# Encoder layer: the fourth tile's norm ahead of the first products, a split between the first MLP pair's prompt products, and weight loads in eight pieces beside the dilated heads

## The chip, the cores and the metric

The kernel runs on one core of a Trainium2 chip. The metric is the device time of one execution in microseconds (us). Names of engines: TensorE (PE) does the matrix products and the transposes, ScalarE (ACT) activations and copies out of the product banks, VectorE (DVE) and GpSimd (POOL) the elementwise work, SyncE (SP) issues most of the loads and stores. Each engine runs its own list of instructions in order, and waits where an operand, a buffer or a transfer isn't ready.

## The reference, cut to what matters

One encoder layer on a sequence of 1024 tokens (sample) and one of 256 (prompt), 1024 channels, everything in float32. An input projection gives queries, keys and values of two attention branches and two sets of gates; the branches are merged through the gates, projected, added to the input, and followed by an MLP of width 4096 and a last norm.

```python
def _layer(x, rel_bias, g_mix, w_in, b_gate, ...):
    h = _rmsnorm(x, g_mix)
    z = h @ w_in
    ...
    gates = jax.nn.sigmoid((z[..., o6:] + b_gate).astype(jnp.float32)).astype(x.dtype)
    ...
    o_a, _ = _banded_attention(qa, ka, va, A_WINDOW, 1, rel_bias[:, :A_HEADS], sink)
    o_b = _dilated_mixture(qb, kb, vb, rel_bias[:, A_HEADS:])
    merged = gates[:, :, 0] * (o_a.reshape(b, S, A_Q) @ w_branch_a) + gates[:, :, 1] * (o_b @ w_branch_b)
    x = x + merged @ w_out
    h = _rmsnorm(x, g_mlp)
    return x + jnp.square(jax.nn.relu(h @ w_up)) @ w_down
```

`_dilated_mixture` is attention of 12 heads in three groups with strides of 1, 4 and 16 tokens, each within a window. The outputs are the two sequences after a last `_rmsnorm`.

## The kernel before

**Tiling.** The 1280 tokens are ten tiles of 128 rows: 0 to 7 are the sample, 8 and 9 the prompt. A float32 operand of a product is split in two parts, `hi` (a rounded copy, made by ACT) and `lo` (the rest, `src - hi`, made by DVE), and one product is three matrix products: hi·hi, hi·lo and lo·hi. So a weight goes through a load (`raw`), ACT (`whi`) and DVE (`wlo`) before PE can use it.

**Seven products.** The sample's part of the large projections runs by Strassen's method in Winograd's form: two column blocks of 128 weights make a pair, and the four quarters of the pair are combined to `ta` and `tb` (L389, four subtractions of halves) and multiplied in seven steps (`seven`) with seven combinations of the activations. The order of the steps in a pair is A11, A12, the prompt's product, S2, S3, S1, A22, S4, and the prompt's second product. `right_pair` (L370) is a generator that makes the weights of the next pair: first the loads, then the splits and subtractions, one piece of work for each `next`. The pair before calls it between its own steps.

**Order.** Nearly all parts of the program run in an order written out by hand (`manual_schedule` on all engines): what stands first in the code stands first in each engine's list. The edits change this order or the loads at three places.

*The start* (values stage, L824 to L860). `square(t)` (L732, L734) sums the squares of tile t and takes the root on ACT, `scale(t)` (L738, L739) makes the normed rows `xn` on DVE, and `turn(t)` transposes them on PE and splits the result in `hhi` (ACT, L765) and `hlo` (DVE, L767); for tiles 0 to 3 four plain copies `a` follow on ACT (L778, L779). PE then multiplies tile after tile with the value weights (L794). The tiles `xt` are loaded by SP at the very start.

*The pairs beside the dilated heads* (`pair`, L1016). There are 14 pairs of columns of the input projection. The last five (`MIXED` = 9, `late` true) run beside the dilated attention: after each step of a pair, `beside` gives the attention generator `attention_b` a turn, in which it issues loads of values (`v`, from `scr_v`, L524), computes scores (`sc`, L537) and products (`pv`, L582), and issues loads of queries and keys (`qk`, from `scr_qb` and `scr_kb`, L509 and L512) for a later turn. All these loads and the weight loads (L377) go through SP in one order. Where a load's buffer isn't free yet, or an earlier transfer of the small set of semaphores in rotation hasn't landed, SP waits, and so does everything behind it. Four of these pairs load weights for the next one, two loads of 512 KB each between S2 and S3.

*The first pair of the MLP* (`up`, L1895, with j = 0). It computes its prompt products at the end instead of after A12, so that they come after the first two steps of the next pair (`begin`). `relu2` writes the squared positive part in two ACT operations; for each prompt product that is two blocks of 128 columns and four small operations (`prompt_out`). Then POOL makes four sums (L1946 to L1949) and SP stores the seven results. The weights of pair 1 are made with the subtractions on DVE (`vector` is true for j = 1), and `steps_of(b, 2)` at the head of the next `up` makes the next splits.

Of the kernel before, what the change touches and what calls it, by code (L numbers as in the profile page):

```python
# [15 lines left out]
P = 128  # L16
D = 1024
KC = D // P
# [19 lines left out]
A11, A12, S2, S3, S1, A22, S4 = range(7)  # L38
# [59 lines left out]
def encoder_kernel(  # L98
# [5 lines left out]
    nc = tc.nc  # L104
# [31 lines left out]
    def bank(tag, name=None):  # L136
        return psum.tile([P, 512], F32, name=name or tag, tag=tag, bufs={"mm": 3, "sc": 2, "pt": 2, "pv": 1}[tag])
# [185 lines left out]
    def steps_of(gen, n):  # L323
        for _ in range(n):
            next(gen, None)
# [34 lines left out]
    def seven(ps, which, right, sub, first=True, last=True, mid=None):  # L360
        six(ps, [left(which, k) for k in range(4)], each(right, sub), first, last, mid)
# [5 lines left out]
        six(ps[:, :NP], lefts, each(part, None), True, True, mid)  # L367
        return ps

    def right_pair(cols, out, make=wslot, vector=False):  # L370

        raw = [make("raw", (P, KC, P)) for _ in range(2)]
        for i in range(2):
            nc.sync.dma_start(raw[i], cols[i])  # L377
        yield

        def part(src, shape):  # L380
            out.append((wslot("whi", shape, F32R), wslot("wlo", shape, F32R)))
            yield from split_steps(*out[-1], src)

        b11, b21, b12, b22 = raw[0][:, :4], raw[0][:, 4:], raw[1][:, :4], raw[1][:, 4:]
        if vector:
            yield from part(raw[0], (P, KC, P))
        ta, tb = make("ta", (P, 2, 4, P)), make("tb", (P, 2, 4, P))
        for o, x, y in ((tb[:, 0], b12, b11), (ta[:, 1], b22, b12), (ta[:, 0], b22, tb[:, 0]), (tb[:, 1], b21, ta[:, 0])):
            (nc.vector if vector else nc.gpsimd).tensor_tensor(o, x, y, op=ALU.subtract)  # L389
            if vector:  # L390
                yield
        if not vector:
            yield
            yield from part(raw[0], (P, KC, P))
        for src, shape in ((ta, (P, 2, 4, P)), (tb, (P, 2, 4, P)), (raw[1], (P, KC, P))):
            yield from part(src, shape)
# [272 lines left out]
    with ExitStack() as pre:  # L669
# [59 lines left out]
        def square(t):  # L729
            xn[t] = slot("xn")  # L730
            ss = small.tile([P, 1], F32, name="ss")
            nc.scalar.activation(xn[t], xs[t], AF.Square, accum_out=ss)  # L732
            sds[t] = small.tile([P, 1], F32, name="sd")
            nc.scalar.activation(sds[t], ss, AF.Sqrt, bias=eps, scale=1.0 / D)  # L734

        def scale(t):
            rs = small.tile([P, 1], F32, name="rs")
            nc.vector.reciprocal(rs, sds.pop(t))  # L738
            nc.vector.scalar_tensor_tensor(xn[t], xs.pop(t), rs, gm, op0=ALU.mult, op1=ALU.mult)  # L739
# [102 lines left out]
        square(2)  # L842
        scale(2)
        next(turns[0], None)
        pss = [bank("mm", "v") for _ in range(2)]
        for t, i in ((0, 0), (0, 1), (1, 0), (1, 1), (0, 2), (1, 2), (0, 3), (1, 3)):
            if (t, i) == (0, 3):
                next(turns[2])
            values(t, 0, pss[t], range(2 * i, 2 * i + 2))
        next(turns[2])  # L850
        square(3)
        next(turns[1], None)
        scale(3)
        square(4)
        next(turns[2], None)
        nc.vector.memset(tab[BUCKETS:, :], NEG)
# [51 lines left out]
    if True:  # L908
# [104 lines left out]
        def pair(b, parts, cols, nxt, hooks, beside, late):  # L1013

            one, two = (out_of(c) for c in cols)
            x, y = bank("mm", "x"), bank("mm", "y")
            np_ = []
            nb = right_pair([w_in3[:, :, c : c + P] for c in nxt], np_, wslot, late) if nxt else iter(())  # L1020

            def halfway(gen=None):
                beside()
                if late:
                    steps_of(gen or nb, 2)

            def behind():
                beside()
                if not late:
                    steps_of(b, 2)  # L1030

            one.begin()
            seven(x, A11, parts[0], 0, last=False, mid=lambda: halfway(b))
            c1 = stage("c", n=2)
            nc.scalar.activation(c1, x, AF.Copy, scale=one.scale)
            behind()
            seven(y, A12, parts[0], 1, mid=lambda: halfway(b))
            one.sum(0, 512, y, c1)
            behind()
            pa = prompt(parts[0], "mm", lambda: halfway(b))  # L1040
            if not late:
                next(nb, None)
            next(hooks, None)
            one.direct(NS, NP, pa)
            beside()
            seven(x, S2, parts[1], 0, False, False, beside)
            c2 = stage("c", n=2)
            nc.scalar.activation(c2, x, AF.Copy, scale=one.scale)
            behind()
            if late:  # L1050
                next(nb, None)
            z = bank("mm", "z")
            seven(z, S3, parts[1], 1, last=False, mid=beside)
            c7 = stage("c", n=2)
            nc.scalar.activation(c7, z, AF.Copy, scale=two.scale)
            two.begin()
            beside()
            next(hooks, None)
            seven(x, S1, parts[2], 0, False, False, beside)
            two.sum(512, 512, x, c7)  # L1060
            beside()
            if not late:
                steps_of(nb, 3)
            next(hooks, None)
            seven(z, A22, parts[2], 1, False, mid=halfway)
            one.sum(512, 512, z, c2)
            one.store()
            beside()
            next(hooks, None)
            seven(x, S4, parts[3], 1, False, mid=halfway)  # L1070
            two.direct(0, 512, x)
            beside()
            two.direct(NS, NP, prompt(parts[3], "mm", halfway))
            two.store()
            beside()
            return nb, np_
# [786 lines left out]
    with ExitStack() as pre:  # L1863
# [25 lines left out]
        def up(j, b, parts, hooks):  # L1889

            def prompt_out(ps, dst):
                for i, d in enumerate(dst):
                    relu2(d[:, 512:], ps[:, P * i : P * i + P])  # L1895

            u = [stage(f"u{i}", TH) for i in range(7)]
            u11, u12, u22, u21 = u[A11], u[A12], u[A22], u[S3]
            start = begin(parts)
            if j not in begun:  # L1900
                next(start)
            z = bank("sc", "z")
            nb = np_ = None
            steps_of(b, 2)
            next(hooks, None)
            x, y, c1 = begun[j] if j in begun else next(start)
            relu2_sum(u11[:, :512], y, c1)
            steps_of(b, 2)
            if j:
                pa = prompt(parts[0])  # L1910
            if j + 1 < FF // P // 2:
                np_ = []
                nb = right_up(j + 1, np_)
                next(nb)
            next(hooks, None)
            seven(x, S2, parts[1], 0, False, False)
            c2 = stage("c2", 512)
            nc.scalar.activation(c2, x, AF.Copy)
            if j:
                prompt_out(pa, (u11, u21))  # L1920
            steps_of(b, 2)
            next(hooks, None)
            seven(z, S3, parts[1], 1, last=False)
            c7 = stage("c7", 512)
            nc.scalar.activation(c7, z, AF.Copy)
            if not j:
                steps_of(nb, 2)
            next(hooks, None)
            seven(x, S1, parts[2], 0, False, False)
            relu2_sum(u22[:, :512], x, c7)  # L1930
            next(hooks, None)
            if nb and j:
                steps_of(nb, 3)
            seven(z, A22, parts[2], 1, False)
            relu2_sum(u21[:, :512], z, c2)
            next(hooks, None)
            if not j:
                *_, begun[1] = begin(np_)
            seven(x, S4, parts[3], 1, False)
            relu2(u12[:, :512], x)  # L1940
            next(hooks, None)
            if not j:
                steps_of(nb, 4)
                prompt_out(prompt(parts[0]), (u11, u21))
            prompt_out(prompt(parts[3], "sc"), (u12, u22))
            nc.gpsimd.tensor_tensor(u[S1], u21, u22, op=ALU.add)  # L1946
            nc.gpsimd.tensor_tensor(u[S2], u[S1], u11, op=ALU.subtract)
            nc.gpsimd.tensor_tensor(u[S3], u11, u21, op=ALU.subtract)
            nc.gpsimd.tensor_tensor(u[S4], u12, u[S2], op=ALU.subtract)  # L1949
            for i in (A11, S1, A22, S2, S3, A12, S4):  # L1950
                nc.sync.dma_start(scr_u[j // 4][:, i, j % 4, :], u[i])
            next(hooks, None)
            return nb, np_
# [47 lines left out]
```

## Time and profile before

| | us |
|---|---|
| timed runs | 1692.21, 1692.16, 1690.64 |
| median | 1692.16 |
| the profiled execution's own time | 1693.05 |
| its span, from the first to the last instruction | 1691.3 |

A row of a timeline gives the start in us, the length in us, the engine, the line, the operation and its operands (out<-in), and how often it stands there in a row; in brackets the idle time of the engine just before it and what ended that. Rows of SP show issues, not transfers. Rows such as "raw<-in_w_in_dram SPq DMA_DIRECT2D x2, 512.0 KB, 8.3" give the number of loads issued in a stretch, the size of one and the median us from issue to landing. Matrix products are pipelined, so that starts can lie closer together than a product is long.

### The profile page before, as it was taken

The numbers are of one execution on the slowest core, as the hardware profiler recorded it, in microseconds if no ns is written. First come the engines' busy times: TensorE is split into PE (matmuls) and PEld (weight loads), VectorE is DVE, ScalarE is ACT, GpSimd is POOL, SyncE is SP. The second block draws the span as 40 slices with busy tenths as digits, with TensorE's granted clock in tenths as the row PEclk, the third lists the DMA queues.
The fourth block names the chain that finished last, engine by engine and source line by source line (L and its number), as shares of the span: only waits on it lengthen the run. The fifth ranks groups of instructions, "written<-read, shape, count | busy, mean of one in ns | idle before, by whom it ended". The sixth has DMA issues, their size and how long they took to land.

```text
span 1691.3 us, 24932 instructions
## 1 busy us (share of the span) xinstructions
PE 1670.7 (99%) x9268; PEld 1414.9 (84%) x9268; DVE 950.1 (56%) x1548; ACT 721.3 (43%) x1489; POOL 514.9 (30%) x404
## 2 busy tenths in 40 slices
PE   8999999999999999999999999999999999999998
PEld 7898888887788888888888888888887888888886
DVE  6733233455563565667378445455457767667575
ACT  6332323356562656654176333333334333333345
POOL 1312212212112472200100556455556322314150
PEclk9999999999999999999999999999999999999999
DMA  7416562567666893845121443343346744633333
GB/s 246 151 57 125 134 136 75 162 192 200 182 196 193 219 245 100 289 136 189 41 85 58 159 159 118 121 159 130 116 152 250 280 152 157 209 106 116 119 119 124
DMA packets 224408, 260.35 MB, mean 154 GB/s; under 512 B 29568, under 2 KB 154288, under 8 KB 224288
## 3 DMA queue, kind: packets, MB, share of 16 engines
q1 hardware_dynamic: 214976, 235.60, 43.9%
q0 software_dynamic: 7936, 20.54, 5.6%
q10 hardware_dynamic: 1376, 2.62, 0.4%
q8 instruction: 73, 1.20, 0.3%
q14 instruction: 47, 0.39, 0.1%
HBM read 173.03 MB, written 90.92 MB: 156 GB/s over the span
## 4 chain that ended last, share of the span: by engine, by line
PE 90%; DVE 4%; ACT 2%; DMA 2%; issue 1%; POOL 1%; SPq 0%; DVEq 0%; ACTq 0%; POOLq 0%
PE dn L347 20%; PE x L347 18%; PE mm L192 14%; PE z L347 9%; PE v L794 6%; PE mm L347 5%; PE y L347 5%; PE sc L347 2%; PE pv L347 2%; PE sc L537 1%; PE pv L1170 1%; PE pv L582 1%; PE pt L569 1%; PE pt L1155 1%; PE sc L1131 1%
## 5 line engine op out<-in xcount | busy, mean ns | idle before, releaser
L347 PE MATMUL dn<-dhi,ulo 128*128 128x512 f32 x448 | 175.7, 392 | 4.3 <-DVE ulo L186 4.3
L347 PE MATMUL dn<-dlo,uhi 128*128 128x512 f32 x448 | 175.2, 391 | 0.0
L347 PE MATMUL dn<-dhi,uhi 128*128 128x512 f32 x448 | 175.1, 391 | 0.0
L347 PE MATMUL x<-chi,wlo 128*128 128x512 f32 x424 | 167.3, 395 | 1.7 <-DVE wlo L314 1.6
L347 PE MATMUL x<-clo,whi 128*128 128x512 f32 x424 | 165.7, 391 | 0.1
L347 PE MATMUL x<-chi,whi 128*128 128x512 f32 x424 | 165.1, 389 | 0.0
L314 DVE TENSOR_TENSOR wlo<-ta,whi 128x1024 fp32r<-128x1024 f32 x30 | 55.7, 1857 | 179.1 <-ACT whi L312 179.1
L314 DVE TENSOR_TENSOR wlo<-raw,whi 128x1024 fp32r<-128x1024 f32 x60 | 92.5, 1541 | 96.7 <-ACT whi L312 96.7
L389 POOL TENSOR_TENSOR tb<-raw 128x512 f32<-128x512 f32 x25 | 32.7, 1308 | 364.4 <-DMA raw<-in_w_in_dram 147.8
L347 PEld LDWEIGHTS dn<-dhi,ulo 128*128 128x128 f32 x448 | 84.6, 189 | 23.2 <-DVE ulo L186 5.7
L186 DVE TENSOR_TENSOR ulo<-uraw,uhi 128x1024 fp32r<-128x1024 f32 x56 | 94.3, 1702 | 12.4 <-ACT uhi L185 12.4
L347 PEld LDWEIGHTS dn<-dhi,uhi 128*128 128x128 f32 x448 | 84.7, 189 | 17.8
L347 PEld LDWEIGHTS dn<-dlo,uhi 128*128 128x128 f32 x448 | 84.7, 189 | 17.4
L347 PEld LDWEIGHTS x<-chi,wlo 128*128 128x128 f32 x424 | 79.8, 188 | 18.1 <-DVE wlo L314 1.3
L347 PEld LDWEIGHTS x<-chi,whi 128*128 128x128 f32 x424 | 79.6, 188 | 17.0
L1699 POOL TENSOR_TENSOR t<-raw,t 128x1024 f32<-128x1024 f32 x16 | 47.7, 3001 | 147.0 <-DMA raw<-in_w_down_dram 147.0
L347 PEld LDWEIGHTS x<-clo,whi 128*128 128x128 f32 x424 | 79.8, 188 | 14.8 <-DVE clo L314 0.4
L1853 DVE TENSOR_TENSOR v<-v,dn 128x512 f32<-128x512 f32 x90 | 59.6, 681 | 40.4 <-PE dn L347 37.9
L1946 POOL TENSOR_TENSOR u<-u,u 128x640 f32<-128x640 f32 x16 | 26.1, 1630 | 160.0 <-ACT u L1871 160.0
L347 PE MATMUL dn<-dhi,up 128*128 128x512 f32 x224 | 73.5, 389 | 0.0
L347 PE MATMUL z<-chi,wlo 128*128 128x512 f32 x184 | 72.0, 391 | 0.0
L272 ACT ACTIVATE pt<-pt 128x512 f32<-128x512 f32 (+1 forms) x70 | 37.9, 543 | 79.5 <-PE pt L1155 45.0
(325 smaller groups left out, 4660.9 us busy)
## 6 DMA issues: line engine op xcount, KB each, us to landing
scr_u<-u SPq DMA_DIRECT2D x112, 320.0 KB, 2.6
uraw<-scr_u SPq DMA_DIRECT2D x56, 512.0 KB, 4.5
raw<-in_w_in_dram SPq DMA_DIRECT2D x33, 512.0 KB, 5.4
raw<-in_w_up_dram SPq DMA_DIRECT2D x32, 512.0 KB, 5.2
raw<-in_w_down_dram SPq DMA_DIRECT2D x28, 512.0 KB, 6.6
sg<-scr_g SPq DMA_DIRECT2D x32, 256.0 KB, 6.4
uraw<-scr_u SPq DMA_DIRECT2D x28, 256.0 KB, 4.7
v<-scr_v SPq DMA_DIRECT2D x96, 64.0 KB, 2.7
```

Of the source, the lines that this page charges most:

```text
L186: nc.vector.tensor_tensor(lo, src, hi.bitcast(F32), op=ALU.subtract)
L192: nc.tensor.matmul(ps, a, b, start=i == 0, stop=i == len(seq) - 1)
L272: nc.scalar.activation(out, in_, AF.Copy)
L314: nc.vector.tensor_tensor(lo, src, hi.bitcast(F32), op=ALU.subtract)
L347: nc.tensor.matmul(ps, a, b, start=first and i == 0, stop=last and i == len(seq) - 1, skip_group_check=True)
L389: (nc.vector if vector else nc.gpsimd).tensor_tensor(o, x, y, op=ALU.subtract)
L537: nc.tensor.matmul(at(k, h)[p0 : p0 + nq, :], qk[rows, p0 : p0 + nq], qk[rows, P + P * a : P + P * a + W], start=True, stop=True, skip_gro ...
L569: nc.tensor.transpose(ps[:, P * a : P * a + P], s[:, h, P * k : P * k + P], ident)
L794: nc.tensor.matmul(ps[:, :n], a, b, start=k == 0 and j == 0, stop=k == KC - 1 and j == 2)
L1699: nc.gpsimd.tensor_tensor(o, a, b, op=ALU.subtract)
L1853: nc.vector.tensor_tensor(v, v, ps, op=ALU.add)
L1946: nc.gpsimd.tensor_tensor(u[S1], u21, u22, op=ALU.add)
```

## The change

Three edits, each at one of the places above.

1. In the start, `square(3)` and `scale(3)` stand ahead of the loop over the first products instead of behind it.
2. In `pair`, the weights of the next pair come in eight loads of 128 KB (two of the eight blocks of rows each) instead of two of 512 KB. They are issued one by one: one after the prompt's product, two around S2's second half, two around S3, three around S1. The subtractions and splits behind them keep their places.
3. In `up` with j = 0, two steps of the next pair's weights are made between the two prompt products, instead of later.

```diff
--- before.py
+++ after.py
@@ -367,15 +367,19 @@
         six(ps[:, :NP], lefts, each(part, None), True, True, mid)
         return ps

-    def right_pair(cols, out, make=wslot, vector=False):
+    def right_pair(cols, out, make=wslot, vector=False, step=KC):

         raw = [make("raw", (P, KC, P)) for _ in range(2)]
         for i in range(2):
-            nc.sync.dma_start(raw[i], cols[i])
-        yield
+            for c in range(0, KC, step):
+                nc.sync.dma_start(raw[i][:, c : c + step, :], cols[i][:, c : c + step, :])
+                if step < KC:
+                    yield
+        if step == KC:
+            yield

         def part(src, shape):
             out.append((wslot("whi", shape, F32R), wslot("wlo", shape, F32R)))
@@ -842,15 +846,15 @@
         square(2)
         scale(2)
         next(turns[0], None)
+        square(3)
+        scale(3)
         pss = [bank("mm", "v") for _ in range(2)]
         for t, i in ((0, 0), (0, 1), (1, 0), (1, 1), (0, 2), (1, 2), (0, 3), (1, 3)):
             if (t, i) == (0, 3):
                 next(turns[2])
             values(t, 0, pss[t], range(2 * i, 2 * i + 2))
         next(turns[2])
-        square(3)
         next(turns[1], None)
-        scale(3)
         square(4)
         next(turns[2], None)
         nc.vector.memset(tab[BUCKETS:, :], NEG)
@@ -1017,7 +1021,7 @@
             one, two = (out_of(c) for c in cols)
             x, y = bank("mm", "x"), bank("mm", "y")
             np_ = []
-            nb = right_pair([w_in3[:, :, c : c + P] for c in nxt], np_, wslot, late) if nxt else iter(())
+            nb = right_pair([w_in3[:, :, c : c + P] for c in nxt], np_, wslot, late, 2 if late else KC) if nxt else iter(())

             def halfway(gen=None):
                 beside()
@@ -1028,6 +1032,14 @@
                 beside()
                 if not late:
                     steps_of(b, 2)
+
+            def piece():
+                if late:
+                    next(nb, None)
+
+            def piece_beside():
+                beside()
+                piece()

             one.begin()
             seven(x, A11, parts[0], 0, last=False, mid=lambda: halfway(b))
@@ -1042,24 +1054,27 @@
                 next(nb, None)
             next(hooks, None)
             one.direct(NS, NP, pa)
+            piece()
             beside()
-            seven(x, S2, parts[1], 0, False, False, beside)
+            seven(x, S2, parts[1], 0, False, False, piece_beside)
             c2 = stage("c", n=2)
             nc.scalar.activation(c2, x, AF.Copy, scale=one.scale)
             behind()
-            if late:
-                next(nb, None)
+            piece()
             z = bank("mm", "z")
-            seven(z, S3, parts[1], 1, last=False, mid=beside)
+            seven(z, S3, parts[1], 1, last=False, mid=piece_beside)
             c7 = stage("c", n=2)
             nc.scalar.activation(c7, z, AF.Copy, scale=two.scale)
             two.begin()
             beside()
+            piece()
             next(hooks, None)
-            seven(x, S1, parts[2], 0, False, False, beside)
+            seven(x, S1, parts[2], 0, False, False, piece_beside)
             two.sum(512, 512, x, c7)
             beside()
-            if not late:
+            if late:
+                steps_of(nb, 2)
+            else:
                 steps_of(nb, 3)
             next(hooks, None)
             seven(z, A22, parts[2], 1, False, mid=halfway)
@@ -1942,6 +1957,7 @@
             if not j:
                 steps_of(nb, 4)
                 prompt_out(prompt(parts[0]), (u11, u21))
+                steps_of(nb, 2)
             prompt_out(prompt(parts[3], "sc"), (u12, u22))
             nc.gpsimd.tensor_tensor(u[S1], u21, u22, op=ALU.add)
             nc.gpsimd.tensor_tensor(u[S2], u[S1], u11, op=ALU.subtract)
```

The first place is ACT in the start. Names: `xn,ss<-xt` is the sum of squares, `sd<-ss,eps` the root, `a_...<-tr` the plain copies of a turned tile. Before:

```order
L778 ACTIVATE a_307<-tr 128x2x128
L779 ACTIVATE a_309<-tr 128x2x128
L778 ACTIVATE a_308<-tr 128x2x128
L779 ACTIVATE a_310<-tr 128x2x128
L765 ACTIVATE hhi<-tr 128x2x128 x4
L732 ACTIVATE xn,ss<-xt 128x1024
L734 ACTIVATE sd<-ss,eps 128x1
L778 ACTIVATE a_307<-tr 128x2x128
L779 ACTIVATE a_309<-tr 128x2x128
```

and now:

```order
L782 ACTIVATE a_307<-tr 128x2x128
L783 ACTIVATE a_309<-tr 128x2x128
L782 ACTIVATE a_308<-tr 128x2x128
L783 ACTIVATE a_310<-tr 128x2x128
L736 ACTIVATE xn,ss<-xt 128x1024
L738 ACTIVATE sd<-ss,eps 128x1
L769 ACTIVATE hhi<-tr 128x2x128 x4
L782 ACTIVATE a_307<-tr 128x2x128
L783 ACTIVATE a_309<-tr 128x2x128
```

The sum of squares and the root of the fourth tile, which stood behind the four `hhi` copies of the third, stand ahead of them. On DVE `rs<-sd` and `xn` move ahead of the third tile's `hlo` in the same way.

The second place is SP in the third of the four pairs that load weights (names with numbers are arrays in memory: `scr_qb_120` and `scr_kb_126` the queries and keys of the group without stride, `scr_g` columns of a gate). Before, from the load of queries and keys ahead of the weights:

```order
L923 DMA scr_g_134<-z 128x256
L524 DMA v<-scr_v 128x128 x2
L509 DMA qk<-scr_qb_120 128x128
L509 DMA qk<-scr_kb_126 128x256
L509 DMA qk<-scr_qb_120 128x128
L509 DMA qk<-scr_kb_126 128x256
L377 DMA raw<-in_w_in_dram 128x8x128 x2
L524 DMA v<-scr_v 128x128 x2
L509 DMA qk<-scr_qb_120 128x128
L509 DMA qk<-scr_kb_126 128x256
L509 DMA qk<-scr_qb_120 128x128
L509 DMA qk<-scr_kb_126 128x256
```

and now:

```order
L378 DMA raw<-in_w_in_dram 128x2x128
L927 DMA scr_g_134<-z 128x256
L528 DMA v<-scr_v 128x128 x2
L513 DMA qk<-scr_qb_120 128x128
L513 DMA qk<-scr_kb_126 128x256
L513 DMA qk<-scr_qb_120 128x128
L513 DMA qk<-scr_kb_126 128x256
L378 DMA raw<-in_w_in_dram 128x2x128 x2
L528 DMA v<-scr_v 128x128 x2
L513 DMA qk<-scr_qb_120 128x128
L513 DMA qk<-scr_kb_126 128x256
L513 DMA qk<-scr_qb_120 128x128
```

Where 1 MB was issued ahead of the two loads of `v`, two pieces of 128 KB stand there now, one stands ahead of the store and the group before, and two, then three more, follow behind the next two groups of queries and keys (not shown).

The third place is ACT in the first pair of the MLP, from its prompt products to the next pair's (`pv` and `sc` are the banks of the two prompt products, `c` a copy of a product, kept for a later sum). Before:

```order
L1870 ACTIVATE u_9308<-pv 128x128
L1871 ACTIVATE u_9308<-u_9308 128x128
L1870 ACTIVATE u_9306<-sc 128x128
L1871 ACTIVATE u_9306<-u_9306 128x128
L1870 ACTIVATE u_9310<-sc 128x128
L1871 ACTIVATE u_9310<-u_9310 128x128
L312 ACTIVATE whi<-ta 128x1024
L312 ACTIVATE whi<-tb 128x1024
L1918 ACTIVATE c_9637<-x 128x512
L1870 ACTIVATE u_9578<-pv 128x128
```

and now:

```order
L1885 ACTIVATE u_9332<-pv 128x128
L1886 ACTIVATE u_9332<-u_9332 128x128
L312 ACTIVATE whi<-ta 128x1024
L1885 ACTIVATE u_9330<-sc 128x128
L1886 ACTIVATE u_9330<-u_9330 128x128
L1885 ACTIVATE u_9334<-sc 128x128
L1886 ACTIVATE u_9334<-u_9334 128x128
L312 ACTIVATE whi<-tb 128x1024
L312 ACTIVATE whi<-raw 128x1024
L1933 ACTIVATE c_9665<-x 128x512
```

`whi<-ta` now stands ahead of the four operations on `sc`, and `whi<-raw`, which stood four operations later, follows `whi<-tb`. On DVE the same pair's rows were:

```order
L389 TENSOR_TENSOR tb<-raw,ta 128x512
L314 TENSOR_TENSOR wlo<-ta,whi 128x1024
L1874 TENSOR_TENSOR u_9578<-y,c_9475 128x512
L1875 SCALAR_TENSOR_TENSOR u_9578<-u_9578 128x512
L314 TENSOR_TENSOR wlo<-tb,whi 128x1024
L314 TENSOR_TENSOR wlo<-raw,whi 128x1024
```

and are now:

```order
L393 TENSOR_TENSOR tb<-raw,ta 128x512
L314 TENSOR_TENSOR wlo<-ta,whi 128x1024
L314 TENSOR_TENSOR wlo<-tb,whi 128x1024
L1889 TENSOR_TENSOR u_9606<-y,c_9499 128x512
L1890 SCALAR_TENSOR_TENSOR u_9606<-u_9606 128x512
L314 TENSOR_TENSOR wlo<-raw,whi 128x1024
```

The `wlo` of `tb` stands ahead of the two operations on `u`, the first of which adds `y` and `c`.

## The prediction

> **What bounds the kernel now.** I read the page first, then the list of what TensorE (PE) waits for, then the timelines around those waits.
>
> ```profile
> span 1691.3 us, 24932 instructions
> PE 1670.7 (99%) x9268; PEld 1414.9 (84%) x9268; DVE 950.1 (56%) x1548; ACT 721.3 (43%) x1489; POOL 514.9 (30%) x404
> ```
>
> PE is busy 1670.7 us of a span of 1691.3 us. The diff leaves PE's list of instructions alone, in number and order, so all that it can take away is time in which PE waits: 20.6 us in the whole program, and a large gain is excluded. The other engines are far from full, so work that moves on them costs nothing unless PE waits for it. The list of waits has four on which an edit of the diff bears, and I take them site by site. Each term is the idle time of PE ahead of one row; the row's bracket gives it and what ended it. A stop costs a little more than its idle time: in PE's rows of site 2 below, products that start 0.22 us apart (456.50, 456.72) are followed by a start at 458.96, so 2.24 − 0.22 = 2.02 us are lost for 1.85 us of idle. I add 0.15 us for each stop that goes away whole.
>
> **Site 1, the start: the fourth tile's norm.** Rows of PE:
>
> ```profile
> 26.23 1.06 PE L338 MATMUL tr<-ident,xn 128*128 128x128 f32 x8 [1.10 <-DVE tab L856]
> ```
>
> of ScalarE (ACT):
>
> ```profile
> 21.99 1.21 ACT L765 ACTIVATE hhi<-tr 128x256 fp32r<-128x256 f32 x4 [4.30 <-PE tr L338]
> 23.06 1.08 ACT L732 ACTIVATE xn<-xt 128x1024 f32<-128x1024 f32 x1
> 24.27 0.29 ACT L734 ACTIVATE sd<-ss,eps 128x1 f32<-128x1 f32 x1
> ```
>
> of VectorE (DVE):
>
> ```profile
> 22.68 1.42 DVE L767 TENSOR_TENSOR hlo<-tr,hhi 128x256 fp32r<-128x256 f32 x4 [3.43 <-ACT hhi L765]
> 24.79 1.28 DVE L739 SCALAR_TENSOR_TENSOR xn<-xt,rs,gm 128x1024 f32<-128x1024 f32 x1
> ```
>
> and of the loads of x, issued by SyncE (SP), with their median time from issue to landing:
>
> ```profile
> 4.41 3.68 SPq L682 DMA_DIRECT2D xt<-in_x_sample_dram  x4
> xt<-in_x_sample_dram SPq DMA_DIRECT2D x4, 512.0 KB, 10.9
> ```
>
> The transposes at 26.23 need the fourth tile's `xn`, finished at 24.79 + 1.28 = 26.07 (the label `tab` names a tiny operation that ended next to it). Before that, ACT squares (1.08) and takes the root (0.29), both behind four `hhi` copies that wait for the third tile's transposes. After the change these stand ahead of the `hhi` copies. ACT sat idle 4.30 us there, DVE 3.43 us, so 1.08 + 0.29 = 1.4 us on ACT and then 1.28 us on DVE are covered, if the tile has landed: it is the second of four loads issued over 3.68 us, so about 4.41 + 0.92 + 10.9 = 16.2 us, ahead of ACT's idle time, which runs from 17.7 to 21.99. DVE then ends `xn` near 19.25 + 1.3 to 20.7, six microseconds early, and `hlo` at 22.68 isn't delayed. The whole wait goes: **1.10 + 0.15 = 1.25 us**. If the tile came as late as the copies, the moved work would stand in front of `hhi`, which the third tile's products need, and would cost up to 1.4 us instead; 16.2 against 21.99 rules that out. What is late next is the fifth tile's `xn`, and its `square` moves up with the rest.
>
> **Site 2, the dilated heads: weights in pieces.** SP issues the loads in order, and an issue that waits holds up those behind it. Its rows:
>
> ```profile
> 448.23 1.05 SPq L377 DMA_DIRECT2D raw<-in_w_in_dram  x2
> 449.38 5.00 SPq L524 DMA_DIRECT2D v<-scr_v  x2
> ...
> 454.90 0.42 SPq L509 DMA_DIRECT2D qk<-scr_kb  x1
> 455.85 0.42 SPq L509 DMA_DIRECT2D qk<-scr_kb  x1
> ```
>
> PE's rows there:
>
> ```profile
> 453.11 0.66 PE L582 MATMUL pv<-pt,v 128*64 128x128 f32 x8
> ...
> 456.50 0.39 PE L347 MATMUL z<-hlo,whi 128*128 128x512 f32 x1
> 456.72 0.39 PE L347 MATMUL z<-hhi,whi 128*128 128x512 f32 x1
> 458.96 1.28 PE L537 MATMUL sc<-qk 64*128 64x256 f32 x8 [1.85 <-DMA qk<-scr_kb]
> ```
>
> And the median times from issue to landing, of what was issued in 446 to 449, in 454 to 456, and in 340 to 505:
>
> ```profile
> raw<-in_w_in_dram SPq DMA_DIRECT2D x2, 512.0 KB, 8.3
> qk<-scr_kb SPq DMA_DIRECT2D x2, 128.0 KB, 3.8
> qk<-scr_kb SPq DMA_DIRECT2D x36, 128.0 KB, 3.0
> ```
>
> Two things make this `qk` late. The `v` load ahead of it holds SP for 5.00 us until the products at 453.11 have released its buffer; that stays. And the two weight loads issued at 448.23, 1 MB together, take 8.3 us and are still draining when `qk` goes out, so that it lands after 3.8 us instead of 3.0. After the change only two 128 KB pieces stand there, a quarter of the bytes, and at a quarter of the 8.3 us they are gone before 453. The issues stay at 454.90 and 455.85. The first half of the scores needs the first of these tiles, the second half, 0.64 us on (half of 1.28), the other. Landing in 3.0 us, they are there at 457.9 and 458.85, which lets the scores start between 457.9 and 458.2: 0.75 to 1.06 us saved. Landing in 2.5 us, it is 1.25 to 1.56. If 3.8 is what such a load takes there anyway, nothing is saved. I take **1.0 us**, by the median of all 36 loads of this kind, and leave 0 to 1.9 for the range.
>
> This happens in one of four pairs; in the others the weights cost PE nothing. All four pay for the pieces: 8 issues in place of 2, 24 more in all, at about 0.45 us each on SP (the x2 and x1 rows above: 0.42 to 0.53), or 24 × 0.45 = 11 us of SP, never of PE, unless a `qk` behind them is late. The tightest places, by rows of SP, the landing of what was issued in 400.8 to 401.9, and rows of PE:
>
> ```profile
> 401.30 0.58 SPq L509 DMA_DIRECT2D qk<-scr_kb  x1
> ...
> 417.55 1.95 SPq L512 DMA_DIRECT2D qk<-scr_kb  x1
> ```
>
> ```profile
> qk<-scr_kb SPq DMA_DIRECT2D x1, 128.0 KB, 4.2
> ```
>
> ```profile
> 405.89 1.13 PE L537 MATMUL sc<-qk 64*128 64x256 f32 x8
> ...
> 423.14 0.67 PE L537 MATMUL sc<-qk 64*64 64x128 f32 x16
> ```
>
> At 405.89 the last `qk` left at 401.30 and landed 4.2 us on, at 405.5; the second half of the scores needs it at 406.45, a margin of 0.95. One piece now stands ahead: 0.45 us of SP, and 128 KB more to drain, about 0.5 us at the eighth of 8.3 / 2. That uses the margin up and no more. At 423.14 three pieces stand ahead: 1.35 us of SP, against 417.55 + 1.95 + 2.5 = 422.0 (its issue waited, so I count from its end) and a margin of 1.1 to the start. The wait inside those 1.95 us shrinks when the issue comes later, which gives some of it back. I allow **+0.3 us** for all four pairs; bounds 0 and the sum in the third rival.
>
> [...]
>
> **Site 3, first pair of the MLP: a split between two prompt products.** Rows of ACT, of DVE and of PE:
>
> ```profile
> 926.94 0.28 ACT L1870 ACTIVATE u<-sc 128x128 f32<-128x128 f32 x1 [1.75 <-PE sc L347]
> 927.98 1.04 ACT L312 ACTIVATE whi<-ta 128x1024 fp32r<-128x1024 f32 x1
> ```
>
> ```profile
> 929.05 1.75 DVE L314 TENSOR_TENSOR wlo<-ta,whi 128x1024 fp32r<-128x1024 f32 x1 [4.74 <-ACT whi L312]
> 933.79 0.69 DVE L1874 TENSOR_TENSOR u<-y,c 128x512 f32<-128x512 f32 x1 [2.98 <-POOL u L1948]
> ...
> 935.76 1.21 DVE L314 TENSOR_TENSOR wlo<-tb,whi 128x1024 fp32r<-128x1024 f32 x1
> ```
>
> ```profile
> 930.86 0.50 PE L347 MATMUL x<-chi,wlo 128*128 128x512 f32 x1 [1.08 <-DVE wlo L314]
> ...
> 937.12 0.47 PE L347 MATMUL x<-chi,wlo 128*128 128x512 f32 x1 [0.48 <-DVE wlo L314]
> ```
>
> PE waits twice here for a `wlo`. The first, of `ta`, ends at 929.05 + 1.75 = 930.8, because its `whi` stands on ACT behind four small operations that wait for PE. After the change `whi<-ta` runs in ACT's idle 1.75 us ahead of 926.94 (it needs 1.04) and DVE, idle 4.74 us, follows at once: `wlo` by about 926.3 + 1.2 = 927.5, two microseconds before PE needs it at 930.86 − 1.08 = 929.8. The small operations aren't delayed, since 925.2 + 1.04 is still ahead of 926.94, and POOL starts on time. The second `wlo`, of `tb`, stood on DVE behind `u<-y,c`, which waits 2.98 us for POOL. It now stands in front: `whi` is done by 927.98 + 1.04 = 929.0, `wlo` by 930.3 (1.2 alone) or 932.5 (3.5, twice the slower 1.75, beside POOL); it is needed at 936.6. `u<-y,c` and its partner then go at 933.79 as before, and nothing of PE waits on them there. Both waits go whole: **1.08 + 0.48 + 2 × 0.15 = 1.9 us**.
>
> **The sum.** −1.25 − 1.0 + 0.3 − 1.9 = −3.85 us. The profiled execution took 1693.05 us, so 1689.2 against it; it is the slowest of those shown, 0.9 above the median of 1692.16 of the timed runs, and against that median it is **1688.3 us**, 0.23% faster. About 0.2% (3.4 us) is what a measurement of this kernel can tell from no change, so the forecast lies close above that line.
>
> **The rivals.**
>
> *First: site 2 keeps its wait.* For it: the issue is held by PE's own products at 453.11, which the pieces don't touch, and pieces are in flight there as well. Against: 3.8 us beside a median of 3.0. Then −1.25 − 1.9 + 0.3 = −2.85: 1689.3 us, within 0.2%.
>
> *Second: all four waits go.* If `qk` lands within 2.2 us of its issue and the tight places hold: −1.25 − 2.0 − 1.9 = −5.15: 1687.0 us.
>
> *Third, the other side: pieces make `qk` late.* One mechanism: each piece pushes the `qk` issues behind it by 0.45 us and their data by about 0.5 us, and a `qk` that is later than its margin stops PE. With 0.95 us per piece, three pieces cost 2.85 against the 1.1 us of margin at 423.14, so 1.75 us; one costs 0.95 against the 0.95 at 405.89. At 1.5 us for each pair, a little under that worst place, four pairs make 6 us, and the net is 6 − 1.25 − 1.9 = +2.85: 1695.0 us, slower. It decides from the point where the added delay beats the margin in most pairs. Against: the two 512 KB loads it replaces put the same bytes into the same stretch, and PE doesn't stop in three of four pairs.
>
> **How the numbers follow.** Forecast 0.48 (1688.3), first rival 0.25 (1689.3), second 0.14 (1687.0), third 0.13 (1695.0, with lesser forms from 1691 up). The runs of before differ by 1692.21 − 1690.64 = 1.6 us, so I count ±0.8 about each. Faster by over 0.2% means below 1688.8: 0.34 of the forecast's 0.48, 0.13 of the second, a quarter of the first (0.07): 0.54. Slower by over 0.2%, above 1695.5, is the worse half of the third: 0.07. The rest, 0.39, is within 0.2%. The range goes from 1686.5, half a microsecond below the second rival, to 1691.3, two above the first: it leaves out the third and little else.
>
> **What would show it.** Site 1: no idle time ahead of the transposes after the third pair of products, and `square` in ACT's idle time. Site 3: both `x<-chi,wlo` starts without a bracket, `wlo<-ta` near 1.2 us. Site 2: the wait at 458.96 cut to about 1 us, and no new PE wait on `qk` or on `wlo` between 340 and 505; the landing of `qk` there near 3.0. The prediction is wrong if new waits for `qk` of over 1 us in sum appear, if the raw pieces come too late for their subtractions, or if any of the first and third sites' waits stays.

## The result, and the profile after

The changed kernel took 1688.56 us (median of 15 runs, 1685.87 to 1691.12), the kernel before, run beside it, 1692.45 us (15 runs, 1690.56 to 1695.35). The ratio is 0.9975, with a 95% interval from 0.9968 to 0.9983: by it 4.2 us faster, between 2.9 and 5.4; the medians differ by 3.9. The forecast was 1688.3. The profiled execution took 1688.49 us. From its page:

```profile
span 1686.7 us, 24976 instructions
PE 1669.5 (99%) x9268; PEld 1414.7 (84%) x9268; DVE 952.5 (56%) x1548; ACT 721.6 (43%) x1489; POOL 511.7 (30%) x404
```

The list of what TensorE waits for (us in all, times, longest) is now:

```profile
PE dn L347 <- DVE ulo L186: 4.3, 3, 3.2
PE tr L338 <- DVE xn L743: 1.8, 2, 0.9
PE warm L711 <- POOL ident masks.py:199: 1.4, 1, 1.4
PE mm L192 <- DVE wlo L235: 1.0, 1, 1.0
PE v L798 <- DVE vlo L705: 0.7, 1, 0.7
PE mm L192 <- ACT z L999: 0.5, 1, 0.5
```

The four waits that the edits aim at (`tab`, `qk` and twice `wlo` of L314) are gone. Two new ones stand there, `wlo` of L235 (1.0) and `z` (0.5), both at places that no edit touches, at 702 and 539 us. To see what is chance in this, the time between the starts of the same two TensorE instructions is taken in every profile; a stretch is named by the times at which these stand in the first profile of the kernel before. From that profile to this one the stretch 14–30 us (site 1) lost 16.02 − 14.72 = 1.30 us, 345–510 (site 2) 1.74, and 925–945 (site 3) 2.15; 510–710 grew by 1.80, and 1290–1310, which no edit touches, lost 1.19. Together 4.58 of the 4.6 us between the spans.

**Site 1.** Rows of ACT and of DVE in the changed kernel, and TensorE's transposes:

```profile
17.53 1.08 ACT L736 ACTIVATE xn<-xt 128x1024 f32<-128x1024 f32 x1
...
18.73 0.29 ACT L738 ACTIVATE sd<-ss,eps 128x1 f32<-128x1 f32 x1
21.96 1.21 ACT L769 ACTIVATE hhi<-tr 128x256 fp32r<-128x256 f32 x4 [2.94 <-PE tr L338]
```

```profile
19.34 1.29 DVE L743 SCALAR_TENSOR_TENSOR xn<-xt,rs,gm 128x1024 f32<-128x1024 f32 x1
22.65 1.42 DVE L771 TENSOR_TENSOR hlo<-tr,hhi 128x256 fp32r<-128x256 f32 x4 [2.02 <-ACT hhi L769]
```

```profile
24.95 1.03 PE L338 MATMUL tr<-ident,xn 128*128 128x128 f32 x8
```

The square has no wait of its own, so the tile had landed; `xn` ends at 20.63 (forecast: up to 20.7), ACT's idle time ahead of `hhi` shrinks from 4.30 to 2.94, and `hhi` itself isn't later. The transposes carry no bracket.

**Site 3.** ACT, DVE and PE:

```profile
923.85 1.04 ACT L312 ACTIVATE whi<-ta 128x1024 fp32r<-128x1024 f32 x1
925.70 0.28 ACT L1885 ACTIVATE u<-sc 128x128 f32<-128x128 f32 x1 [0.80 <-PE sc L347]
```

```profile
924.93 1.23 DVE L314 TENSOR_TENSOR wlo<-ta,whi 128x1024 fp32r<-128x1024 f32 x1 [1.87 <-ACT whi L312]
927.81 1.76 DVE L314 TENSOR_TENSOR wlo<-tb,whi 128x1024 fp32r<-128x1024 f32 x1 [1.66 <-ACT whi L312]
932.55 0.69 DVE L1889 TENSOR_TENSOR u<-y,c 128x512 f32<-128x512 f32 x1 [2.98 <-POOL u L1964]
```

```profile
928.38 0.40 PE L347 MATMUL x<-chi,wlo 128*128 128x512 f32 x1
```

`whi<-ta` fills ACT's idle time, both `wlo` are there 2.2 us and more before TensorE asks for them, and the long wait of DVE for POOL (2.98) still stands, with nothing of TensorE behind it. The second `wlo`, which runs while POOL makes its sums, takes 1.76 us, the first, without POOL, 1.23.

**Site 2.** SP in the changed kernel, at the place of the wait:

```profile
447.59 1.57 SPq L378 DMA_DIRECT2D raw<-in_w_in_dram  x2
449.26 0.94 SPq L528 DMA_DIRECT2D v<-scr_v  x2
450.29 0.41 SPq L513 DMA_DIRECT2D qk<-scr_qb  x1
450.80 0.38 SPq L513 DMA_DIRECT2D qk<-scr_kb  x1
```

```profile
456.05 1.13 PE L541 MATMUL sc<-qk 64*128 64x256 f32 x8
```

The wait is gone whole, and not for the reason that the prediction gave: the `v` loads, which held SP for 5.00 us before, now take 0.94, so `qk` (`scr_kb`) leaves at 450.80 instead of 454.90. Of these 4.1 us, 1.3 are the lead that TensorE has from site 1; by the other 2.8 us `qk` is earlier than the products that need it. What of this the pieces did, the experiments tell.

### The profile page after: what moved, and what is told of

Its sections match the earlier page's. It is cut to its first block, busy times and chain, and to the rows that moved or that the text cites. A ratio compares the mean times of both kernels' runs of the same rounds, so it can differ in the third digit from the quotient of the medians.

```text
span 1686.7 us, 24976 instructions
## 1 busy us (share of the span) xinstructions
PE 1669.5 (99%) x9268; PEld 1414.7 (84%) x9268; DVE 952.5 (56%) x1548; ACT 721.6 (43%) x1489; POOL 511.7 (30%) x404
## 4 chain that ended last, share of the span: by engine, by line
PE 91%; DVE 4%; ACT 2%; DMA 1%; issue 1%; POOL 0%; SPq 0%; DVEq 0%; ACTq 0%; POOLq 0%
PE dn L347 20%; PE x L347 18%; PE mm L192 14%; PE z L347 9%; PE v L798 6%; PE mm L347 5%; PE y L347 5%; PE pv L347 3%; PE sc L347 2%; PE pv L1185 2%; PE sc L541 1%; PE pv L586 1%; PE pt L573 1%; PE pt L1170 1%; PE sc L1146 1%
## 5 line engine op out<-in xcount | busy, mean ns | idle before, releaser
L314 DVE TENSOR_TENSOR wlo<-ta,whi 128x1024 fp32r<-128x1024 f32 x30 | 55.2, 1840 | 173.0 <-ACT whi L312 173.0
L314 DVE TENSOR_TENSOR wlo<-raw,whi 128x1024 fp32r<-128x1024 f32 x60 | 90.9, 1516 | 96.3 <-ACT whi L312 96.3
L393 POOL TENSOR_TENSOR tb<-raw 128x512 f32<-128x512 f32 x25 | 32.3, 1290 | 368.4 <-DMA raw<-in_w_in_dram 127.6
L347 PE MATMUL z<-chi,whi 128*128 128x512 f32 x184 | 71.6, 389 | 0.0
```

Of the source, the lines that this page charges most:

```text
L314: nc.vector.tensor_tensor(lo, src, hi.bitcast(F32), op=ALU.subtract)
L347: nc.tensor.matmul(ps, a, b, start=first and i == 0, stop=last and i == len(seq) - 1, skip_group_check=True)
```

## The experiments

Three questions: what each edit is worth alone, whether what stood at site 2 and behind it belongs to the kernels or to one execution, and by what the weight loads reach TensorE.

**Each edit alone, and the whole again.** The first adds the two `square(3)`/`scale(3)` lines of the diff alone, the second the pieces alone, the third `steps_of(nb, 2)` alone; the fourth is the changed kernel unaltered.

> The fourth tile's norm alone. Theory: the wait of 1.10 us ahead of the transposes goes, TensorE is 1.26 us ahead from there on, the other three waits stay: 1.3 us less, ratio 0.9992. By theory A on the later waits (transfers that keep their own time) a part of it is lost again at 702, where the kernel before had about 0.1 us of slack: then 0.1 to 0.5 us in the end. Rival: another wait near the start grows by as much, ratio 1.000.

> The eight pieces alone. Theory from the profile after: the wait of 1.85 us goes whole (2.06 us with its slower restart) and 0.3 us come back at the scores before it: 1.8 us less by 460, ratio 0.9990 if it reaches the end, 0.9996 if the stretch at 702 takes 1.1 us of it. Prediction on record: 0.7 us less. Rival: pieces alone, without the earlier TensorE of the first part, meet a different state of the transfers and a part of the wait stays (0.8 us or more at that place).

> The split between the first MLP pair's prompt products alone. Theory: both waits on wlo (1.08 and 0.48 us) go, 2.1 us with the slower restarts, and nothing behind it is bound by transfers: 2.1 us less at the end, ratio 0.9988, no change at all ahead of 925 us. Rival: the long wait on ulo (3.2 us) takes a part of it: then that wait is 4 us or more and the end only 1 us earlier, ratio 0.9994.

> The changed kernel once more, for a second profile. In the first one TensorE had two waits that the kernel before hasn't: 0.52 us on ScalarE's z<-x at 539.4 and 0.97 us on wlo at 702.3, together 1.5 us given back of what the three sites had won by then. Theory A: they belong to the change (TensorE comes 2.4 to 3 us earlier to stretches whose transfers keep their own time); then both are there again, 0.5 and 1.0 us. Theory B: they are chance in the transfers of one execution; then at least one is gone or of another size. In both the four waits of before (1.10, 1.85, 1.08, 0.48 us) stay away, and the time is 0.9975 of before, within 0.0008.

Measured, against 1692.33 us of the kernel before: norm alone 1690.58, ratio 0.9988 (0.9979 to 0.9997); split alone 1690.54, 0.9986 (0.9977 to 0.9995); pieces alone 1692.21, 0.9997 (0.9988 to 1.0005); the whole again 1687.24, 0.9968 (0.9956 to 0.9981). The profiles are sharper than the times:

```
us between the same TensorE instructions
                      14-30   345-510   510-710   925-945   1290-1310
before                16.02   164.94    200.02    20.11     20.01
norm alone            14.73   163.45    199.14    20.11     18.22
split alone           16.01   163.35    200.61    17.96     18.79
pieces alone          16.02   163.27    201.48    20.09     18.87
changed               14.72   163.20    201.82    17.96     18.82
changed, again        14.72   162.87    200.28    17.96     18.85
```

Sites 1 and 3 are exact: 1.3 and 2.15 us whenever the edit is in, nothing when it isn't. Site 2 isn't. Norm alone and split alone load the weights as before, and the long wait on `qk` isn't there: 0 and 0.29 us at that place instead of 1.85. The two later waits of the changed kernel (0.52 and 0.97) were 0.17 and 0 in its second profile, and 0.51 and 0.47 with the pieces alone: theory B.

**The kernel before once more, and the two other edits without the pieces.**

> The kernel before once more, for a second profile. The stretch from 447 to 465 us (by the first profile's times, at the same instruction of TensorE) took 18.02 us there, with the 1.85 us wait; in the two kernels without pieces (norm alone, split alone) it took 16.24 and 16.44, in the three with pieces 15.96 to 16.36. Theory C: the long wait was chance in the transfers of one execution; then 16.2 to 16.6 us now. Theory D: it belongs to the exact times of this kernel and an earlier or later TensorE avoids it; then about 18.0 us again. The waits at the start (1.10) and of wlo (1.08, 0.48) are there in both.

> The first and third edit without the pieces. Theory C (pieces worth nothing that shows): stretches 385 to 505 as in the changed kernel within 0.4 us, ratio 0.9975 as the whole change. Theory by the prediction's terms: pieces worth 0.7 us, ratio 0.9979; by the first profile's 1.8 us, ratio 0.9986. In all of them 3.4 us less at the two sites.

The kernel before took 1692.0 us, ratio 1.000 (0.999 to 1.001). From 447 to 465 it needed 16.68 us instead of 18.02, with a wait of 0.51 us where 1.85 had been (and one of 0.28 at 412, so that 345–510 took 164.16); TensorE's waits for `wlo` (1.09, 0.51) and ahead of the transposes (1.09) were all there. So most of the 1.85 us was chance in the transfers: theory C. The two edits without the pieces took 1688.3 us, ratio 0.9975 (0.9964 to 0.9986), the same as with them, and 163.41 in the stretch.

**What the loads do to SP.** Two kernels without pieces otherwise (first and third edit are in):

```diff
 (whole loads at the first piece's place)
             one.direct(NS, NP, pa)
+            if late:
+                next(nb, None)
             beside()
...
             behind()
-            if late:
-                next(nb, None)
 (eight pieces in a row at the old place)
-            nc.sync.dma_start(raw[i], cols[i])
+            for c in range(0, KC, step):
+                nc.sync.dma_start(raw[i][:, c : c + step, :], cols[i][:, c : c + step, :])
```

> As the one without pieces, but the two whole loads of 512 KB go where the changed kernel issues its first piece, ahead of a place with 0.95 us of margin. If bytes ahead in the queue make qk late (the mechanism that the prediction gives for site 2), 1 MB more to drain there stops TensorE in most of the four pairs: 0.5 to 3 us in each, 3 to 8 us in all, ratio 0.999 to 1.003. If transfers share the engines and qk passes beside the weights, nothing is seen: under 0.5 us, ratio 0.9975 to 0.998.

> As the one without pieces, but the weights come as eight pieces issued in a row at the old place: the same bytes at the same place, six SyncE issues more (2.7 us of SP in each pair). [...] If only late qk issues count, SP catches up during its wait for the v buffer and nothing is seen, ratio 0.9975 to 0.998.

The whole loads put ahead of the tight place took 1696.27 us, ratio 1.0029 (1.0017 to 1.0042): 0.54% or 9 us slower than the same kernel with the loads at their old place. The stretch 345–510 grew from 163.41 to 172.82. Its waits for `qk` in the list, and TensorE at the first of the two long ones (1.86 us; the other took 2.65):

```profile
PE sc L537 <- DMA qk<-scr_kb: 5.9, 5, 2.7
```

```profile
408.16 1.35 PE L537 MATMUL sc<-qk 64*128 64x256 f32 x8 [1.86 <-DMA qk<-scr_kb]
409.44 1.03 PE L582 MATMUL pv<-pt,v 128*64 128x64 f32 x16
410.40 1.97 PE L569 MATMUL pt<-ident,s 128*128 128x128 f32 x8
```

So weights ahead of a `qk` can cost 9 us in this stretch; 5.9 of it is idle time, and behind the first of the two long waits 1.8 us more were lost at a lower clock (below). The pieces in a row took 1691.87 us, ratio 0.9996 (0.9987 to 1.0006), 3.6 us slower than the whole loads at the same place, and even their fastest run (1690.78) is slower than every run of that kernel beside it (at most 1689.24). Where the 3.6 us go isn't found: the profile shows 1.4 of them in 345–510 (164.82), in two waits for `qk` at 411 and 412, and that is no more than the stretch takes with whole loads in some profiles (163.35 to 164.94). Here is SP, first with the whole loads (no pieces, first and third edit), then with the eight in a row:

```profile
447.82 1.15 SPq L377 DMA_DIRECT2D raw<-in_w_in_dram  x2
449.07 2.57 SPq L524 DMA_DIRECT2D v<-scr_v  x2
451.74 0.38 SPq L509 DMA_DIRECT2D qk<-scr_qb  x1
```

```profile
448.20 4.14 SPq L378 DMA_DIRECT2D raw<-in_w_in_dram  x8
452.44 0.89 SPq L525 DMA_DIRECT2D v<-scr_v  x2
453.42 0.38 SPq L510 DMA_DIRECT2D qk<-scr_qb  x1
```

Behind two loads of 512 KB the two `v` issues took 2.57 to 5.00 us of SP in all six profiles with the loads at that place (5.00, 3.87, 3.45, 3.61, 2.57, 3.22), behind loads of 128 KB 0.89 to 1.36, at most 0.50 more than two such issues took at 398.89 in the first profile of the kernel before (0.86). In the kernel before itself, run a second time, the first `v` went out at 453.35, a microsecond ahead of the end of the products that the prediction took for its release (454.44); in the four other kernels with the loads at that place it was 1.3 to 1.8 us ahead. Nor was it an earlier transfer whose semaphore this load uses again: in all six profiles that transfer had landed before the hold began (in the first one of before it landed at 447.69, and the hold began at 449.38). Eight pieces in a row cost about as much in issue time (4.14) as the hold did: `qk` leaves 5.22 us after the first of the weights, against 3.92 with the whole loads here (3.92 to 6.23 in the six) and 2.70 in the changed kernel, where only two pieces stand there.

**Once more with and without, four pieces, and another order of two splits.** The four pieces are `step = 4`, one at each of the places after the prompt's product and in the middle of S2, S3 and S1. The last kernel is the changed one with one more edit, which goes at TensorE's longest wait:

```diff
+            self.left(*JOBS[0], 0)
+            self.left(*JOBS[0], 1)
             self.right(*JOBS[0], slot)
             self.combine(*JOBS[1])
             yield
-            self.left(*JOBS[0], 0)
-            self.left(*JOBS[0], 1)
             yield
```

> The changed kernel a third time, beside the next one. Sum of TensorE's time from 345 to 510 us (by the first profile's times, the same instructions): with pieces so far 163.20, 162.87, 163.27; without 164.94, 164.16, 163.45, 163.35, 163.41. If the pieces are worth the difference of the means (0.75 us) by taking away chance waits on qk, this one lies at 162.9 to 163.3 again, and the time within 1.5 us of the one without pieces.

> The first and third edit without the pieces, a second time. If weights ahead in the queue make qk late now and then, the sum from 345 to 510 us lies between 163.3 and 165, above every profile with pieces; if the pieces are worth nothing, below 163.3. The start (14 to 30 us) takes 14.7 and the MLP's first pairs (925 to 945) 17.96 us in both theories; ratio 0.997 to 0.998.

> The changed kernel with four pieces of 256 KB instead of eight of 128 KB, one at each of the first four places of the pieces. If what counts is bytes ahead of a qk with little margin (heaped whole loads there cost 9 us), 256 KB at the first place cost 0.3 to 1 us a pair, so the sum from 345 to 510 is 164 to 166. If what counts is the number of issues (heaped pieces cost 1.4 us), it is 163.0 or less.

> The changed kernel, with the two splits of the second MLP projection's first left operand (uhi, ulo) moved ahead of the splits of its right operand. TensorE waits 3.2 us for ulo there in every profile, and the products behind it start 0.43 instead of 0.23 us apart for a while; DVE makes ulo behind dlo, u<-z,c and beside POOL's subtraction. If that order is the cause, the wait goes or falls under 1 us and the stretch from 1290 to 1310 falls from 18.8 to 14 or 15 us: 4 us less than the changed kernel, ratio 0.995. If the load of uraw or POOL sets it, the wait stays at 2 to 3 us, ratio 0.997.

The changed kernel took 1688.18 us, ratio 0.9974 (0.9965 to 0.9984); without the pieces 1688.87, 0.9974 (0.9965 to 0.9984); four pieces 1688.65, 0.9974 (0.9962 to 0.9986). None differs from another. In 345–510 the changed kernel missed its expectation: 165.51, with waits for `qk` at two new places. One is the place at which three pieces stand ahead, which the prediction's third rival named:

```profile
421.96 0.45 PE L541 MATMUL sc<-qk 64*64 64x128 f32 x8
424.06 0.45 PE L541 MATMUL sc<-qk 64*64 64x128 f32 x8 [1.65 <-DMA qk<-scr_kb]
```

Without the pieces it was 163.45, with four 162.97, and with eight and the other order of splits 162.87, which is a stretch without any wait. Over all profiles: without pieces 164.94, 164.16, 163.45, 163.35, 163.41, 163.45, mean 163.79; with eight pieces 163.20, 162.87, 165.51, 163.27, 162.87, mean 163.54. The difference of 0.25 us is much less than the spread of either. The expectations don't settle it: 163.45 is not below 163.3, and 162.97 with four pieces is below 163.0, which speaks, narrowly, for a small worth of the pieces and against a cost by bytes; 165.51 speaks against that worth. Four of the five profiles with eight pieces lie below all six without, and the fifth above them all. A gain of some tenths of a microsecond, lost again now and then, is possible and not shown.

The other order of splits took 1684.37 us, ratio 0.9953 (0.9941 to 0.9965): 8 us faster than the kernel before, and some 4 us faster than the changed one. Its waits for `ulo` in the list and DVE's rows show why:

```profile
PE dn L347 <- DVE ulo L186: 2.7, 4, 0.8
```

```profile
1286.12 3.96 DVE L186 TENSOR_TENSOR ulo<-uraw,uhi 128x1024 fp32r<-128x1024 f32 x2 [0.52 <-ACT uhi L185]
1290.01 2.35 DVE L186 TENSOR_TENSOR dlo<-t,dhi 128x1024 fp32r<-128x1024 f32 x2
```

In the changed kernel the same two had stood behind `dlo` and the sums, beside POOL's subtractions:

```profile
1292.64 6.68 DVE L186 TENSOR_TENSOR ulo<-uraw,uhi 128x1024 fp32r<-128x1024 f32 x2
1292.50 5.74 POOL L1714 TENSOR_TENSOR t<-raw 128x1024 f32<-128x1024 f32 x2 [3.93 <-DMA raw<-in_w_down_dram]
```

Now `ulo` runs in a gap of DVE, ahead of `dlo` and of the second product's sums, and only the first 1.75 of its 3.96 us are beside a subtraction. The 3.2 us wait goes, 1290–1310 falls from 18.8 to 13.49 us, and 2.9 us of that come back between 1310 and 1600, in three waits of 0.6 to 0.8 us for later `ulo`.

## Why the prediction was right, point by point

**The sum was right, one of its three terms was not.** Forecast 1688.3, measured 1688.56. What carries the 4.2 us are sites 1 and 3, 1.30 + 2.15 = 3.45 us in every profile; the pieces bring nothing that these runs can tell from none. That the sum came within 0.3 us of the time is in part luck: sites 1 and 3 were forecast at 3.15 and gave 0.3 more, and the 0.7 us that the sum has for the pieces (1.0 less 0.3) isn't shown.

**Site 1** (forecast 1.25): 1.30, which is 0.20 beside the idle time of 1.10. Cover, landing of the tile and the end of `xn` were as worked out.

**Site 3** (forecast 1.9): 2.15. Both waits went whole. The size that was off is the 0.15 us added for each stop: the rows of before give 1.08 and 0.48 us of idle time, but TensorE's starts gained 1.39 and 0.77 there, so these stops cost 0.3 us each beside their idle time. Idle time counts from the end of a product, which is 0.16 us longer than the distance between two starts (0.28 against 0.12 and 0.39 against 0.23); that is the 0.15. The rest is lost behind the stop, where the next two starts are 0.34 and 0.31 us apart instead of 0.23.

**Site 2** (forecast 1.0 less 0.3): not shown, 0.25 us by the profiles' means and 0 by the times. Two steps failed. First, the 1.85 us were taken from one execution as a property of the kernel; in the five other profiles with the whole loads at their old place the wait there was 0.51, 0, 0.29, 0 and 0.37. Secondly, "The `v` load ahead of it holds SP for 5.00 us until the products at 453.11 have released its buffer; that stays": it does not. The products' end and the hold's end lay near each other in that one profile; in the five others with whole loads `v` went out 1.1 us and more before these products ended. With pieces the same `v` goes out at 449.26, well ahead of those products (452.12). The hold goes with the two large loads ahead of it: 2.57 to 5.00 us for the two `v` behind them, 0.89 behind the same bytes in eight pieces. What it waits for there no row names, and it is left open.

**The cost of the pieces** (forecast +0.3, third rival up to 6). The margins at 405.89 and 423.14 were read rightly as the tight ones: a wait of 1.65 us came at the second, in one of five profiles. That pieces can cost is shown by the time of the eight in a row (3.6 us, by what path is open), that weights ahead of `qk` can cost more by the whole loads placed early (9 us). The spread-out pieces show neither on the mean. Nor do the 24 transfers more show as an added cost: with them and without them the ratios are 0.9974 and 0.9974.

**The first rival** (site 2 keeps its wait) comes nearest to what happened to that term, for another reason: there was, on the mean, hardly a wait to keep. By it the time was to be 1689.3.

**What the prediction didn't have:** 510–710 varies from 199.1 to 201.8 us between profiles, with short waits that come and go (`z` at 539, `wlo` at 702), and 1290–1310 from 18.2 to 20.3 for one and the same order of instructions. A profile of each kernel, compared as a whole (4.6 us), is right here by luck: 1.74 of site 2 and 1.19 of the last stretch are for the most part chance in the first profile, and 1.80 chance in the second.

## What to carry to other kernels

A wait on a transfer that stands in one profile may be smaller or absent in the next (here 1.85 us in one, 0.51 in the next of the same kernel, 0 in two others that share this part); before a term is built on it, compare the same stretch in a second profile, or in any other kernel that shares this part. The waits on another engine's fixed order, with no transfer in them, repeated here (1.09 to 1.10 us ahead of the transposes, 1.08 to 1.09 for `wlo`, in four profiles each), and moving the work into an idle stretch of that engine gained them whole, with 0.2 to 0.3 us more for each. Where an issue on a queue is held, look at the size of the loads ahead of it before its own buffer is blamed (here 2.57 to 5.00 us behind two loads of 512 KB, 0.89 to 1.36 behind loads of 128 KB).

## What the runs showed of the hardware

Behind some stops of TensorE the granted clock fell to 0.50 in these profiles, and a stop could then cost more than its idle time (3.7 us for 1.86 us of it, below). Windows of the changed kernel around the wait for `ulo` (columns: us, busy time and count of PE, PEld, DVE, ACT and POOL, granted clock, DMA share, GB/s):

```profile
1296.00:1299.00 3.00, 2.93 (x6) 1.82 (x6) 3.00 (x2) 0.75 (x2) 3.00 (x2) 0.50 0.06 23
1299.00:1302.50 3.50, 3.12 (x14) 2.58 (x15) 3.50 (x3) 1.39 (x2) 3.42 (x2) 0.95 0.27 98
```

For about 3 us behind the wait of 3.2 us the granted clock is 0.50, and products start 0.43 us apart instead of 0.23. In the first profile of the kernel before, the clock was still 0.61 over the next 3.5 us, which makes the 1.19 us of chance in this stretch. It isn't so each time, other than the expectation of the last run says. In the thirteen profiles that have this wait (2.7 to 3.2 us) the clock stayed at 1.00 in five, the changed kernel's second (3.22 us of wait) and third among them; in three it was 0.50 for 3.41 us, in five for 6.83. The stretch 1290–1310 took 18.3 to 18.9 us in the first group, 18.2 to 18.9 in the second and 19.7 to 20.3 in the third. So 3.41 us at 0.50 cost nothing here, since the seventh product behind the wait has to wait for a later `ulo` in any case (0.38 us still in the changed kernel, at 1299.38), and the second 3.41 us cost over a microsecond.

A wait of 1.86 us in the kernel with whole loads placed early was followed by a lower clock too, 0.76 and 0.75 on the mean over the next 6.9 us:

```profile
408.10:411.00 2.90, 2.84 (x27) 2.11 (x28) 0.94 (x5) 0.38 (x1) 0.00 (x0) 0.76 0.62 163
411.00:415.00 4.00, 4.00 (x18) 3.48 (x17) 2.23 (x7) 2.56 (x9) 1.60 (x3) 0.75 0.73 189
```

These means hide a step: the trace has 1.00 until 409.58, 0.50 for 3.41 us, and 1.00 again (`x<-chi,wlo` takes 0.78 us at 412.02, 0.40 at 413.25). The wait of 1.85 us at 458.96 in the first profile of the kernel before was not followed by a lower clock:

```profile
458.90:461.00 2.10, 2.04 (x18) 1.33 (x19) 0.76 (x4) 0.13 (x1) 0.00 (x0) 1.00 0.54 138
```

So one stop of this length cost 2.1 us and the other 3.7, by the starts of the same products with and without it; the length alone doesn't tell them apart. Between its changes the clock kept one value for 1293.65, 6.83 and 382.29 us in the first profile of the kernel before (379, 2 and 112 times 3.413), and for 1290.24, 3.41 and 385.71 us in the first of the changed kernel (378, 1 and 113 times). What decides behind which stop it falls isn't shown.
